# Hybrid encoder block on one core: row buffers, weight fetches and the first gated table of the head loop rearranged

## The chip, the cores and the metric

The kernel runs on one core of a Trainium2 chip. The metric is the device time of one execution in microseconds (us); lower is better. The core has a matrix engine (PE in the profile, with its weight loads shown apart as PEld), a vector engine (DVE), a scalar engine (ACT), a general engine (POOL) and a queue engine (SP) that issues most of the transfers. Each of them works through its own list of instructions strictly in order. An instruction that has to wait for another engine or a transfer holds up everything behind it on its own engine.

## The reference

The block prepends 16 learned tokens to a sequence of 1024 tokens of width 1024, applies two residual layers and a last normalization, and drops the learned tokens.

```
h = concat(meta, x)
h = h + token_mixer(rmsnorm(h))     # 4 gated (mLSTM) heads and 4 retention heads
h = h + channel_mixer(rmsnorm(h))   # silu(conv(u @ w_up)) * (u @ w_gate) @ w_down
out = rmsnorm(h)[:, 16:]
```

In the token mixer each of the eight heads has queries and keys of 128 columns, values of 256 columns and an output gate of 256 columns, all of them projections of the normalized input. A head's sequence is processed in chunks with a state carried from chunk to chunk. In a gated head the scores of a chunk are multiplied by a table of weights, exp(log gates), and q and k pass through a convolution over four tokens and a silu. In a retention head the table is a fixed decay, and q and k are rotated. Each head's result is normalized, multiplied by the gate, and all heads together are projected by w_out.

## The kernel before

Single-precision products are made of three reduced-precision ones: every operand is split into a rounded part (hi) and the remainder (lo), and PE computes hi*hi, hi*lo and lo*hi. So each weight block is fetched raw from memory, then **rounded**: ACT copies it to hi, and DVE subtracts to get lo (lines 151 and 152).

The heads run in the order 4, 0, 1, 2, 3, 5, 6, 7: first one retention head, then the four gated heads (0 to 3), then the other retention heads. For each head the program states three stages. In the **gate stage** (`o_group`) PE makes the output gate of the head in two blocks (o0, o1) of three token pieces each, and between these groups the head's scan over the first chunks is placed. In the **value stage** (`v_group`, nine chunks) PE makes the next head's values, and between them come the rest of the scan and `post_steps`: for each of three pieces a square root (line 891), the scaling of the rows (line 898), two transposes on PE (line 906) and the product with the gate. In the **query-key stage** (`qk_group`) PE makes the next head's queries and keys, three pieces each.

The scan step of a chunk (`scan_a`, `scan_b`) multiplies keys with queries on PE (line 796), transposes the keys (line 801), lets ACT scale and round the keys (`kwh`, line 809 in gated heads, 818 in retention heads) and DVE make the remainder (`kwl`), and multiplies both with the values on PE (lines 826 to 828), which gives the output of the chunk and the update of the state (`C`, line 868).

**Weights** come through one list of units, worked off in this order for each head: o0, o1, the rows of w_out for the last two tokens of the previous head (m0, m1), then v0, v1, q, k of the next head. `need(key, ahead)` makes sure that the unit `key` and the next `ahead` units of the list have been issued; to issue a weight unit means its fetch (line 148), and right behind it its rounding. Raw weights go to a ring of two buffers (pool `wraw`), rounded ones to a ring of three. The m units take a buffer of the same ring of two (line 177), are fetched by line 178 and used by DVE alone: each is multiplied into the accumulator `acc` of the last two tokens (lines 181 and 183). The value group of the first chunk (16 tokens) also reads the raw weights (line 367).

**Tables.** `tables(h)` fetches two tables: for a gated head A1 and A2 from a small matrix in memory, spread over all partitions (lines 531 and 532). For A1 POOL then adds the causal mask (lines 535 and 536), and ACT takes the exponential of nine chunks (line 539), the first of 16 columns and eight of 128. For the first gated head the call stands ahead of the head loop, and for the others behind the value stage of the head before.

**Order.** The program's text sets only a priority. A planner lays out each engine's list at build time: by its own estimates of durations it takes, for each engine, what would be ready, the earliest of the text first, subject to data, to buffers that come free, and to a few explicit rules, `after(x, y)`, which place x behind y on the same engine. There is such a rule for each square root of the heads before the last (behind the last gate's activation, line 431) and for the sigmoids of gated heads (behind the last silu).

Of the kernel before, what the change touches and what calls it, by code (L numbers as in the profile page):

```python
# [17 lines left out]
P = 128  # L18
# [6 lines left out]
H = 4  # L25
# [38 lines left out]
def body(ctx, tc, h_in, vecs, cst, mask_in, rot, w_v0, w_v, w_fm, w_out, w_up, w_gate, w_down, out):  # L64
# [56 lines left out]

    units = []
    ready = {}
    issued = [0]

    def unit(key, src, n):
        units.append((key, src, n))
# [4 lines left out]
    def split_tiles(nm):  # L132
        return [wsp.tile([P, UN], F32R, tag=t, name=f"{t}_{nm}") for t in ("hi", "lo")]

    def issue(upto):
        while issued[0] < min(upto, len(units)):
            u = units[issued[0]]
            issued[0] += 1
            if callable(u[1]):
                ready[u[0]] = u[1]()  # L140
                continue
            key, src, n = u
            nm = "_".join(str(k) for k in key)
            raw = raw_tile(nm)
            sub = 2 if key[:2] == ("v", HF) else 1
            cuts = [n * i // sub for i in range(sub + 1)]
            for c0, c1 in zip(cuts, cuts[1:]):
                last["raw"] = nc.sync.dma_start(raw[:, c0:c1], src[:, c0:c1])
            hi, lo = split_tiles(nm)
            for c0, c1 in zip(cuts, cuts[1:]):  # L150
                nc.scalar.copy(hi[:, c0:c1], raw[:, c0:c1])  # L151
                nc.vector.tensor_tensor(lo[:, c0:c1], raw[:, c0:c1], hi[:, c0:c1].bitcast(F32), ALU.subtract)  # L152
            ready[key] = (hi, lo, raw)

    order = {}

    def need(key, ahead):
        if not order:
            order.update({u[0]: i for i, u in enumerate(units)})
        issue(order[key] + 1 + ahead)  # L160
        return ready[key]


# [10 lines left out]
            unit((kind, h, b), w_fm[h, j + b], D)  # L174

    def last_two(k, raw=None):
        raw = raw_tile(f"m{k}") if raw is None else raw
        nc.sync.dma_start(raw[:, :D], w_out[k])
        for t in range(2):
            if k != 2 * HF:  # L180
                nc.vector.scalar_tensor_tensor(acc[:, t], raw[:, :D], mm[:, k, t:t + 1], acc[:, t], ALU.mult, ALU.add)
            else:
                nc.vector.tensor_scalar(acc[:, t], raw[:, :D], mm[:, k, t:t + 1], None, ALU.mult)
# [174 lines left out]
    def v_group(h, c, tag="pp"):  # L358
        t0, L = CH[c]
        nv = 264 if h == HF else 256  # L360
        U = [need(("v", h, i), 2 - i) for i in range(2)]
        pv = pp(f"pv{h}_{c}", tag)
        if c == 0:

            for i in range(2):
                for j in range(4):
                    nc.tensor.matmul(pv[32 * j:32 * j + 32, :nv], ug[:, 4 * i + j, :], U[i][2][:, j * nv:(j + 1) * nv],
                                     start=i == 0, stop=i == 1, tile_position=(0, 32 * j))
            t = wk.tile([P, WMAX], F32, tag="cv", name=f"v0_{h}", bufs=2)[:META]
            nc.scalar.copy(t[:, :nv], pv[:META, :nv])  # L370
            for j in range(1, 4):
                nc.vector.tensor_tensor(t[:, :nv], pv[32 * j:32 * j + META, :nv], t[:, :nv], ALU.add)
            return lambda: v_evac(h, 0, META, t)
        for kb in range(KB):
            hi, lo, _ = U[kb // 4]
            o = (kb % 4) * nv
            a, b = uh[kb][:, t0:t0 + L], ul[kb][:, t0:t0 + L]
            nc.tensor.matmul(pv[:L, :nv], a, hi[:, o:o + nv], start=kb == 0, stop=False)  # L378
            nc.tensor.matmul(pv[:L, :nv], a, lo[:, o:o + nv], start=False, stop=False)  # L379
            nc.tensor.matmul(pv[:L, :nv], b, hi[:, o:o + nv], start=False, stop=kb == KB - 1)  # L380
        return lambda: v_evac(h, c, L, pv)
# [40 lines left out]
    def o_group(h, b, p):  # L422
        t0, t1, _ = PIECES[p]
        t0 = max(t0, KEEP)
        n = t1 - t0
        U = need(("o", h, b), 2)
        pt = pp(f"po{h}_{b}_{p}")
        fm_mms(pt, U, t0, t1)
        s = sig(b, p)
        nc.vector.tensor_tensor(s, pt[:, :n], Rb[:, t0:t1], ALU.mult)  # L430
        x = nc.scalar.activation(s, s, AF.Sigmoid if h < H else AF.Silu)
        if h < H:
            after(x, last["silu"])
        last["gate"] = x
# [86 lines left out]
    def tables(h):  # L521
        if h > H + 1:
            return
        if h >= H:
            nc.sync.dma_start(A2, rot[:, 1])
            nc.sync.dma_start(A1, rot[:, 0])
            return
        src = scr.rearrange("x (c h) t -> x h c t", h=H)
        for x, a in ((0, A1), (1, A2)):
            if x == 0:  # L530
                nc.sync.dma_start(a[:, :META], src[x, h, 0, :META].partition_broadcast(P))
            nc.sync.dma_start(a[:, META:].rearrange("p (c t) -> p c t", t=P), src[x, h, 1:].partition_broadcast(P))
        m = mask
        a = A1[:, META:].rearrange("p (c t) -> p c t", t=P)
        nc.gpsimd.tensor_tensor(A1[:, :META], A1[:, :META], m[:, :META], ALU.add)
        nc.gpsimd.tensor_tensor(a, a, m.rearrange("p (o t) -> p o t", o=1).to_broadcast([P, NCH - 1, P]), ALU.add)
        for c in range(NCH):
            t0, L = CH[c]
            nc.scalar.activation(A1[:, t0:t0 + L], A1[:, t0:t0 + L], AF.Exp, bias=cols[:, 0, c * H + h:c * H + h + 1])

# [332 lines left out]
    def post_steps(h, p):  # L875
        t0, t1, chs = PIECES[p]
        n = len(chs)
        m = {}

        def stats():  # L880
            num, mv, base = outs.pop(p)
            z = mxp.tile([P, 4], F32, tag="z", name=f"z{h}_{p}", bufs=2)
            if h < H:
                den = base[:, 0:n, DV]
                e2 = cols[:, 2].rearrange("p (c h) -> p h c", h=H)[:, h, chs[0]:chs[0] + n]
                nc.vector.tensor_tensor(z[:, :n], den, den, ALU.mult)
                nc.vector.tensor_tensor(z[:, :n], z[:, :n], e2, ALU.max)
                nc.vector.scalar_tensor_tensor(z[:, :n], z[:, :n], EPS, mv[:, 0:n, 1], ALU.mult, ALU.add)
            else:
                nc.vector.tensor_tensor(z[:, :n], mv[:, 0:n, 1], Re[:, h - H, chs[0]:chs[0] + n], ALU.add)  # L890
            x = nc.scalar.activation(z[:, :n], z[:, :n], AF.Sqrt)
            if h < 7:
                after(x, last["gate"])
            nc.vector.reciprocal(z[:, :n], z[:, :n])
            nc.vector.scalar_tensor_tensor(mv[:, 0:n, 1], mv[:, 0:n, 0], -1.0, z[:, :n], ALU.mult, ALU.mult)
            for i, c in enumerate(chs):
                L = CH[c][1]
                nc.scalar.activation(num[i][:L, :DV], num[i][:L, :DV], AF.Identity, bias=mv[:L, i, 1:2], scale=z[:L, i:i + 1])
            m["num"] = num

        def half(b):
            num = m["num"]
            tr = ps.tile([P, 512], F32, tag="tr", name=f"tr{h}_{p}_{b}")
            for i, c in enumerate(chs):
                c0, L = CH[c]
                nc.tensor.transpose(tr[:, c0 - t0:c0 - t0 + L], num[i][:L, b * P:(b + 1) * P], ident[:L, :L])
            a0 = max(t0, KEEP)
            w = t1 - a0
            g = (V_MLG if h < H else V_RTG) + (h % H) * 2 + b
            i = 2 * h + b  # L910

            def mix_into(dst, x0, x1):
                nc.vector.scalar_tensor_tensor(dst, tr[:, x0 - t0:x1 - t0], vec[:, g:g + 1], sig(b, p)[:, x0 - a0:x1 - a0], ALU.mult, ALU.mult)
            if h == 7:
                for q, o in (("A2", MA), ("B2", MB)):
                    x0, x1 = max(a0, o), min(t1, o + HB)
                    if x0 < x1:
                        mix_into(wact(q, 6 + b)[:, x0 - o:x1 - o], x0, x1)
                if t1 > MB + HB:
                    mix_into(mm[:, i], MB + HB, t1)  # L920
                return
            mx = sig(b, p)
            mix_into(mx[:, :w], a0, t1)
            e = min(t1, MB + HB)
            nc.sync.dma_start(mxd[i][:, a0 - MA:e - MA], mx[:, :e - a0])
            if e < t1:
                nc.vector.tensor_copy(mm[:, i], mx[:, e - a0:w])
        return [stats, lambda: half(0), lambda: half(1)]
# [79 lines left out]
    for i, h in enumerate(ORDER):  # L1008
# [8 lines left out]
        merge([lambda c=c: (v_group(nxt, c)(), c == 4 and i == 4 and wsum_next()) for c in range(NCH)], side)  # L1017
        if i:
            tables(nxt)
        for kind in "qk":  # L1020
            for p in range(3):
                qk_group(nxt, kind, p)
# [585 lines left out]
```

## Time and profile before

| What | Value |
|---|---|
| median of three runs | 1547.7 us (1545.21, 1547.7, 1548.02) |
| the profiled execution, its own time | 1545.12 us |
| span of the profiled execution | 1543.3 us |
| PE busy | 1519.3 us (98%) |
| DVE busy / ACT busy | 1089.1 us (71%) / 732.0 us (47%) |
| mean granted clock of PE | 0.995 |

The span runs from the first to the last instruction of the execution; 1.8 us of its time lie around it. A list of waits names for each waiting instruction the engine, the program's name of what it writes and its line, then what released it; the numbers are the sum in us, how many times, and the longest. A timeline row has the start and the duration in us from the start of the span, then engine, line and operation, and in brackets the idle time of the engine just before it with what ended it. A row of windows has, for a stretch of time, its length, the busy time of each engine with the number of instructions, the granted clock of PE, the share of the transfer engines and GB/s.

### The profile page before, as it was taken

Reading aid. Unit: us, or ns where it says so; the run is one execution under the profiler, and the core shown is the slowest. Engines: PE = TensorE matmul, PEld = TensorE weight load, DVE = VectorE, ACT = ScalarE, POOL = GpSimd, SP = SyncE. Lnnn points to the kernel's source line nnn. Section 1 sums busy time; section 2 is a strip of 40 time slices with the busy share of each in tenths; the row PEclk is TensorE's granted clock in tenths of the full one; section 3 lists DMA queues with packets and bytes.
Section 4 is the critical chain, followed back from the end, with each engine's and each line's share of the span. In section 5 each row is a group of like instructions: output and inputs, shape, how many; then the busy total and the mean of one; then the engine's idle time right before and its main releaser. Section 6 shows DMA issues by size and latency. Waiting matters only on the chain.

```text
span 1543.3 us, 25397 instructions
## 1 busy us (share of the span) xinstructions
PE 1519.3 (98%) x9763; PEld 1397.2 (91%) x9763; DVE 1089.1 (71%) x2334; ACT 732.0 (47%) x1488; POOL 101.7 (7%) x117
## 2 busy tenths in 40 slices
PE   8999999999999999999999999999999999999997
PEld 8989999999999999997788998999999999888887
DVE  8757767676867566678867778776666666778657
ACT  7374554544543434436454465444444444434443
POOL 0001010010101000000000000211101110000000
PEclk9999999999999999999999999999999999999999
DMA  6125243452648143357543237889666667933313
GB/s 215 42 70 130 77 123 83 123 117 78 162 109 200 54 119 75 103 116 244 185 137 109 83 99 245 203 220 205 161 151 157 145 160 196 372 101 112 96 42 110
DMA packets 105192, 213.41 MB, mean 138 GB/s; under 512 B 9384, under 2 KB 31600, under 8 KB 105072
## 3 DMA queue, kind: packets, MB, share of 16 engines
q1 hardware_dynamic: 86384, 176.86, 33.8%
q0 software_dynamic: 18544, 34.87, 15.4%
q8 instruction: 76, 1.25, 0.3%
q14 instruction: 44, 0.36, 0.1%
q10 hardware_dynamic: 144, 0.07, 0.0%
HBM read 182.37 MB, written 84.19 MB: 173 GB/s over the span
## 4 chain that ended last, share of the span: by engine, by line
PE 94%; DVE 2%; DMA 2%; ACT 1%; issue 0%; POOL 0%; SPq 0%; DVEq 0%; ACTq 0%; POOLq 0%
PE pv L378 4%; PE pv L379 4%; PE pv L380 4%; PE po L388 4%; PE po L390 4%; PE po L389 4%; PE pdx L557 3%; PE pdx L559 3%; PE pdx L558 3%; PE pup_x L558 2%; PE pup_x L559 2%; PE pga_x L557 2%; PE pga_x L559 2%; PE pga_x L558 2%; PE pup_x L557 2%; PE pdy L557 2%
## 5 line engine op out<-in xcount | busy, mean ns | idle before, releaser
L378 PE MATMUL pv<-hi_v,uh 128*128 128x256 f32 (+1 forms) x512 | 147.5, 288 | 3.0 <-ACT hi_v L151 1.9
L379 PE MATMUL pv<-lo_v,uh 128*128 128x256 f32 (+1 forms) x512 | 146.4, 286 | 0.0
L380 PE MATMUL pv<-hi_v,ul 128*128 128x256 f32 (+1 forms) x512 | 145.3, 285 | 0.0
L388 PE MATMUL po<-uh,hi_o 128*128 128x386 f32 (+2 forms) x384 | 124.8, 325 | 0.0
L389 PE MATMUL po<-ul,hi_o 128*128 128x386 f32 (+2 forms) x384 | 123.4, 321 | 0.0
L390 PE MATMUL po<-uh,lo_o 128*128 128x386 f32 (+2 forms) x384 | 123.3, 321 | 0.0
L378 PEld LDWEIGHTS pv<-hi_v,uh 128*128 128x128 f32 x512 | 97.3, 190 | 6.6 <-issue 2.9
L379 PEld LDWEIGHTS pv<-lo_v,uh 128*128 128x128 f32 x512 | 97.1, 190 | 0.4 <-DVE lo_v L152 0.4
L380 PEld LDWEIGHTS pv<-hi_v,ul 128*128 128x128 f32 x512 | 97.0, 190 | 0.1
L196 POOL DMA_DIRECT2D wsd<-w_down_d x55 | 50.9, 1022 | 570.7 <-DMA wsd<-w_down_d 472.4
L245 ACT CAST hi_up<-raw_up 128x512 fp32r<-128x512 f32 (+1 forms) x52 | 36.5, 720 | 106.6 <-PE pga_z L558 61.2
L389 PEld LDWEIGHTS po<-ul,hi_o 128*128 128x128 f32 x384 | 73.0, 190 | 0.1
L388 PEld LDWEIGHTS po<-uh,hi_o 128*128 128x128 f32 x384 | 72.9, 190 | 0.1
L390 PEld LDWEIGHTS po<-uh,lo_o 128*128 128x128 f32 x384 | 72.8, 190 | 0.1
L246 DVE TENSOR_TENSOR lo_ga<-fraw_ga,hi_ga 128x512 fp32r<-128x512 f32 (+1 forms) x52 | 41.9, 809 | 37.9 <-ACT hi_ga L245 37.6
L557 PE MATMUL pup_x<-uh_g,hi_up 128*128 128x256 f32 (+1 forms) x240 | 67.2, 282 | 0.4 <-ACT uh_g L1039 0.4
L558 PE MATMUL pup_x<-ul_g,hi_up 128*128 128x256 f32 (+1 forms) x240 | 67.4, 283 | 0.1
L246 DVE TENSOR_TENSOR lo_up<-raw_up,hi_up 128x512 fp32r<-128x512 f32 (+1 forms) x52 | 41.4, 809 | 35.7 <-ACT hi_up L245 34.9
L559 PE MATMUL pup_x<-uh_g,lo_up 128*128 128x256 f32 (+1 forms) x240 | 66.3, 282 | 0.0
L388 PE MATMUL pq<-uh,hi_q 128*128 128x400 f32 (+2 forms) x192 | 62.4, 325 | 0.2 <-DVE rq L409 0.2
L388 PE MATMUL pk<-uh,hi_k 128*128 128x400 f32 (+2 forms) x192 | 62.4, 325 | 0.0
L389 PE MATMUL pk<-ul,hi_k 128*128 128x400 f32 (+2 forms) x192 | 62.2, 324 | 0.0
(751 smaller groups left out, 5027.3 us busy)
## 6 DMA issues: line engine op xcount, KB each, us to landing
raw_up<-w_up_d SPq DMA_DIRECT2D x22, 512.0 KB, 6.6
fraw_ga<-w_gate_d SPq DMA_DIRECT2D x22, 512.0 KB, 3.6
acts<-cv SPq DMA_DIRECT2D x44, 256.0 KB, 5.6
wsd<-w_down_d SPq DMA_DIRECT2D x22, 512.0 KB, 7.0
wsd<-w_down_d POOLq DMA_DIRECT2D x22, 512.0 KB, 6.6
rd<-wsd SPq DMA_DIRECT2D x22, 512.0 KB, 3.6
wsd<-w_down_d POOLq DMA_DIRECT2D x33, 256.0 KB, 7.2
raw_o<-w_fm_d SPq DMA_DIRECT2D x16, 512.0 KB, 3.6
```

What stands on the lines that cost most here:

```text
L196: nc.gpsimd.dma_start(x, v, accum_op=ALU.add)
L245: nc.scalar.copy(hi[:, o:o + n], x)
L246: nc.vector.tensor_tensor(lo[:, o:o + n], x, hi[:, o:o + n].bitcast(F32), ALU.subtract)
L378: nc.tensor.matmul(pv[:L, :nv], a, hi[:, o:o + nv], start=kb == 0, stop=False)
L379: nc.tensor.matmul(pv[:L, :nv], a, lo[:, o:o + nv], start=False, stop=False)
L380: nc.tensor.matmul(pv[:L, :nv], b, hi[:, o:o + nv], start=False, stop=kb == KB - 1)
L388: nc.tensor.matmul(pt[:, :n], a, uh[kb][:, t0:t1], start=kb == 0, stop=False)
L389: nc.tensor.matmul(pt[:, :n], a, ul[kb][:, t0:t1], start=False, stop=False)
L390: nc.tensor.matmul(pt[:, :n], b, uh[kb][:, t0:t1], start=False, stop=kb == KB - 1)
L557: m.append(nc.tensor.matmul(pt, ah, xh_, start=first and k == 0, stop=False, skip_group_check=True))
L558: nc.tensor.matmul(pt, ah, xl_, start=False, stop=False, skip_group_check=True)
L559: m.append(nc.tensor.matmul(pt, al, xh_, start=False, stop=last and k == n - 1, skip_group_check=True))
```

## The change

Three things are done.

1. **Row buffers.** The rows of w_out for the last two tokens (m units) no longer take a buffer of the ring of raw weights, but two of their own, one for even and one for odd rows. Those two buffers exist before too, for the sums of the first norm and for a ring of a later stage.
2. **Two points.** A new function `load(upto)` makes the fetches alone, and `issue` the rounding. `need` gets a third argument, the number of units ahead to be fetched. A value group asks for the fetch of three units past v0 and of two past v1 (so up to k), and for the rounding of one unit past v0 in the chunks 0 to 3, and of two (so q) from chunk 4 on; before it was two in each chunk. The groups of the second gate block ask from the second piece on for four units ahead, where they asked for two: m0, m1, v0 and v1.
3. **Exponentials.** The mask addition and the exponentials of a table are a function of their own, `exps(h)`. For the first gated head it is called behind the value stage of head 4, no longer ahead of the head loop; the fetch of the table stays where it was. For gated heads 1 to 3 it follows the fetch as before. And each exponential is bound by a rule behind the last square root that the text states ahead of it (`last["root"]`), in all four tables.

```
     issued, loaded, raws = [0], [0], {}
...
+    def load(upto):
+        while loaded[0] < min(upto, len(units)):
+            key, src = units[loaded[0]][:2]
+            loaded[0] += 1
+            if callable(src):
+                continue
+            n = units[loaded[0] - 1][2]
+            raws[key] = raw = raw_tile("_".join(str(k) for k in key))
+            sub = 2 if key[:2] == ("v", HF) else 1
+            cuts = [n * i // sub for i in range(sub + 1)]
+            for c0, c1 in zip(cuts, cuts[1:]):
+                last["raw"] = nc.sync.dma_start(raw[:, c0:c1], src[:, c0:c1])
...
+            load(issued[0])
...
-            raw = raw_tile(nm)
+            raw = raws.pop(key)
...
-            for c0, c1 in zip(cuts, cuts[1:]):
-                last["raw"] = nc.sync.dma_start(raw[:, c0:c1], src[:, c0:c1])
...
-    def need(key, ahead):
+    def need(key, ahead, loads=0):
...
         issue(order[key] + 1 + ahead)
+        if loads:
+            load(order[key] + 1 + loads)
...
     def last_two(k, raw=None):
-        raw = raw_tile(f"m{k}") if raw is None else raw
+        raw = accp.tile([P, 2 * HB], F32, tag=f"rr{k % 2}", name=f"raw_m{k}") if raw is None else raw
...
-        U = [need(("v", h, i), 2 - i) for i in range(2)]
+        U = [need(("v", h, i), (2 if c > 3 else 1) - i, 3 - i) for i in range(2)]
...
-        U = need(("o", h, b), 2)
+        U = need(("o", h, b), 4 if b and p else 2)
...
+        if h:
+            exps(h)
+
+    def exps(h):
         m = mask
...
-            nc.scalar.activation(A1[:, t0:t0 + L], A1[:, t0:t0 + L], AF.Exp, bias=cols[:, 0, c * H + h:c * H + h + 1])
+            after(nc.scalar.activation(A1[:, t0:t0 + L], A1[:, t0:t0 + L], AF.Exp, bias=cols[:, 0, c * H + h:c * H + h + 1]), last["root"])
...
-            x = nc.scalar.activation(z[:, :n], z[:, :n], AF.Sqrt)
+            x = last["root"] = nc.scalar.activation(z[:, :n], z[:, :n], AF.Sqrt)
...
         if i:
             tables(nxt)
+        else:
+            exps(nxt)
```

More of the change, by code (lines that the diff above doesn't have):

```diff
@@ L123, in body @@
     ready = {}
-    issued = [0]
+    issued, loaded, raws = [0], [0], {}
     def unit(key, src, n):
@@ L142, in issue @@
             key, src, n = u
-            nm = "_".join(str(k) for k in key)
-            raw = raw_tile(nm)
+            raw = raws.pop(key)
             sub = 2 if key[:2] == ("v", HF) else 1
             cuts = [n * i // sub for i in range(sub + 1)]
-            for c0, c1 in zip(cuts, cuts[1:]):
-                last["raw"] = nc.sync.dma_start(raw[:, c0:c1], src[:, c0:c1])
-            hi, lo = split_tiles(nm)
+            hi, lo = split_tiles("_".join(str(k) for k in key))
             for c0, c1 in zip(cuts, cuts[1:]):
```

## The prediction

> **What bounds the kernel now.** I read the page's busy table first, then the windows by stage, then PE's list of waits, and then the timelines around the two places that it names.
>
> ```profile
> span 1543.3 us, 25397 instructions
> PE 1519.3 (98%) x9763; PEld 1397.2 (91%) x9763; DVE 1089.1 (71%) x2334; ACT 732.0 (47%) x1488; POOL 101.7 (7%) x117
> ```
>
> PE is busy for 1519.3 of 1543.3 us. The change leaves every product in place, so it can only take from the 24.0 us in which PE is idle, or from time at a lower clock. The windows say where these lie: columns are the stretch, its length, then the busy time of PE, PEld, DVE, ACT and POOL, and the granted clock.
>
> ```profile
> 90.00:170.00 80.00, 76.70 (x562) 74.04 (x561) 56.63 (x153) 43.64 (x97) 7.92 (x7) 1.00 0.45 112
> 250.00:330.00 80.00, 80.00 (x588) 78.17 (x587) 54.95 (x154) 41.32 (x94) 6.44 (x6) 1.00 0.42 109
> 330.00:410.00 80.00, 77.16 (x557) 74.69 (x556) 53.22 (x152) 45.14 (x99) 6.92 (x7) 0.98 0.37 97
> 900.00:1543.00 643.00, 634.54 (x3746) 560.68 (x3744) 448.57 (x725) 290.03 (x523) 52.33 (x57) 1.00 0.60 166
> ```
>
> The change works in the head loop, some 64 to 740 us. There only two regions within its reach have holes: 3.3 us in 90 to 170 and 2.84 in 330 to 410 (with the clock at 0.98). The quiet stretch 250 to 330 shows that a whole head can pass without a hole. The 8.5 us behind 900 belong to other code. PE's waits name the holes:
>
> ```profile
> PE u L826 <- ACT kwh L809: 2.6, 1, 2.6
> PE u L826 <- DVE C L868: 1.3, 1, 1.3
> PE s L796 <- DVE kwl L819: 1.1, 1, 1.1
> PE pv L378 <- DVE gts L356: 1.0, 1, 1.0
> ```
>
> The first is in head 2's gate stage, the next two at the start of head 0's values, the fourth in the opening. The timeline of the second place:
>
> ```profile
> 97.04 2.38 POOL L536 TENSOR_TENSOR A<-A,mask 128x1024 f32<-128x1024 f32 x1 [9.49 <-DMA A<-scr]
> 98.22 1.05 ACT L151 CAST hi_q<-raw_q 128x1024 fp32r<-128x1024 f32 x1 [3.96 <-DMA raw_q<-w_fm_d]
> 99.28 1.28 ACT L539 ACT_TABLE_LOAD   x1
> 99.30 1.23 DVE L152 TENSOR_TENSOR lo_q<-raw_q,hi_q 128x1024 fp32r<-128x1024 f32 x1 [3.52 <-ACT hi_q L151]
> 100.58 2.45 ACT L539 ACTIVATE A<-A,cols 128x128 f32<-128x128 f32 x8
> 101.01 0.42 DVE L868 SCALAR_TENSOR_TENSOR C<-C,u 128x256 f32<-128x256 f32 x1
> 101.58 0.36 PE L826 MATMUL u<-vh,kwh 128*128 128x256 f32 x1 [1.27 <-DVE C L868]
> 102.93 0.35 ACT L818 ACTIVATE kwh<-s,Rc 128x128 fp32r<-128x128 f32 x1
> 103.72 0.49 PE L796 MATMUL s<-qT,kT 128*128 128x128 f32 x2 [1.07 <-DVE kwl L819]
> ```
>
> ACT stands 3.96 us before the rounding of q, whose raw weights are not there; DVE stands behind it at lo_q, with the state update C queued behind. PE runs dry for 1.27 us. Then ACT does a table load and eight exponentials (1.28 + 2.45 us), with the scan's kwh queued behind, and PE runs dry for another 1.07. The other place:
>
> ```profile
> 321.23 0.33 SPq L148 DMA_DIRECT2D raw_v<-w_v_d  x1
> 330.97 1.05 ACT L151 CAST hi_v<-raw_v 128x1024 fp32r<-128x1024 f32 x1 [13.44 <-DMA raw_v<-w_v_d]
> 331.93 0.53 ACT L415 ACTIVATE kT<-cvk 128x400 f32<-128x400 f32 x1
> 332.05 1.23 DVE L152 TENSOR_TENSOR lo_v<-raw_v,hi_v 128x1024 fp32r<-128x1024 f32 x1 [4.62 <-ACT hi_v L151]
> 336.96 1.28 ACT L431 ACT_TABLE_LOAD   x1
> 338.26 0.94 ACT L431 ACTIVATE sig<-sig 128x386 f32<-128x386 f32 x2
> 339.10 0.35 ACT L809 ACTIVATE kwh<-s,cols 128x128 fp32r<-128x128 f32 x1
> 339.50 0.39 PE L826 MATMUL u<-vh,kwh 128*128 128x258 f32 x1 [2.58 <-ACT kwh L809]
> 339.56 1.28 ACT L539 ACT_TABLE_LOAD   x1
> 340.85 0.31 ACT L539 ACTIVATE A<-A,cols 128x16 f32<-128x16 f32 x1
> 342.11 1.28 ACT L431 ACT_TABLE_LOAD   x1
> ```
>
> ACT waits 13.44 us for the raw values of the next head, DVE 4.62 us behind it; the silus of k, the gate's table load and kwh all come late, and PE waits 2.58 us. (The raw_v of the next head is fetched while the current head's keys are computed, long ahead of its place in the text: the planner runs ahead as far as buffers allow.)
>
> **The clock behind a hole.** Windows right after:
>
> ```profile
> 340.60:344.10 3.50, 3.50 (x13) 3.50 (x12) 1.56 (x2) 3.46 (x7) 0.00 (x0) 0.51 0.00 0
> 344.10:347.60 3.50, 3.50 (x26) 3.50 (x25) 2.97 (x11) 2.09 (x8) 0.00 (x0) 1.00 0.02 5
> ```
>
> For 3.5 us PE was granted 0.51 of its clock and started 13 products, where the next 3.5 us have 26. So the hole costs 3.5 x (1 - 0.51) = 1.7 us more. The Trainium skill (TensorE: Matmul & The Clock Gate, "Why this matters for your kernels") sets the limit at idle gaps of more than about 3 us; by it a hole of 2.58 us would cost only itself, and the sum below would be 1.7 less. The row shows the drop after the shorter hole, so I go by the row.
>
> **Part 1, row buffers.** Today m0 and m1 stand between o1 and v0 in the ring of two, so a value block can be fetched only when DVE has used up an m row; SP stands for that in its fetches (line 148) eleven times.
>
> ```profile
> SPq L148 <- DVE acc L181: 31.6, 11, 3.9
> 313.54 1.04 ACT L151 CAST hi_o<-raw_o 128x1024 fp32r<-128x1024 f32 x1
> 314.94 1.22 DVE L152 TENSOR_TENSOR lo_o<-raw_o,hi_o 128x1024 fp32r<-128x1024 f32 x1
> 323.66 0.34 PE L388 MATMUL po<-uh,hi_o 128*128 128x386 f32 x1
> ```
>
> With buffers of their own, v1 needs only o1's rounding, over at 314.94 + 1.22 = 316.2, and v0 that of o0, which is earlier still; today v0 goes out at 321.23. From issue to use it took 9.7 us today; even at that v0 would be there by about 326, at 316.2 issue, and it is likely earlier. Its rounded buffer is that of k, whose products run until the gate's begin at 323.66, so ACT's wait ends at some 324 to 326 in place of 331: 5 to 7 us earlier, and the chain silu, table load, kwh moves with it. That is more than the 2.58 us that PE waited. Removed: 2.58 and the 1.7 of clock. Lower end: nothing, if another fetch on SP's in-order queue takes the place. No bytes and no instructions are added, only other buffers. What is late next is the piece-by-piece arrival of k from DVE, which the quiet heads show to be covered.
>
> **Part 2, two points.** At 98 us q loses its early place in the text: its rounding is stated at chunk 4, while C of chunk 1 is stated ahead. The planner may still put hi_q into an ACT gap, but DVE should take C ahead of lo_q. I count the 1.27 us as removed; lower end 0 (hi_q and lo_q stay where they are), upper end 1.27. The move of v0 and v1 up into the gate groups raises the rank of two roundings a head (1.05 us ACT and 1.23 DVE each, rows above); they ran there or earlier anyway. Cost 0; the bad end is a rival below. The fetches of q and k still leave when the first chunk has read v's raw buffers, so SP, with the stores and table fetches queued behind, waits there as today: 0. In the opening q's rounding also comes later: it can give back the 1.0 us wait for gts, or cost up to its own 1.05 + 1.23 us if PE then waits for q; I take 0.
>
> **Part 3, exponentials.** The eight exponentials leave 99.28 to 103.03, and kwh need not wait for them: 1.07 us removed, the surest item. In the three other gated boundaries the 16-column exponential is today pulled into the gate stage (339.56 above) and costs ACT two table loads, 2 x 1.28; the rule puts it with the rest. PE does not wait for these two, so 0. What the rule adds is a block of 1.28 + 2.45 = 3.73 us behind the root:
>
> ```profile
> 311.46 0.20 ACT L891 ACTIVATE z<-z 128x2 f32<-128x2 f32 x1
> 312.54 1.10 ACT L898 ACTIVATE num<-num,mv,z 128x256 f32<-128x256 f32 x2 [0.69 <-DVE mv L895]
> 315.65 0.27 PE L906 MATMUL tr<-cs,num 128*128 128x128 f32 x1
> ```
>
> The cover is the 0.69 us gap and the 2.0 us between the end of L898 (313.64) and PE's transpose at 315.65. If all eight go ahead of L898, PE waits 3.73 - 0.69 - 2.0 = 1.0 us in a boundary; with four tables 4 us is the bad end, none the good one. L898 is stated ahead of the exponentials and is ready 0.9 us after the root, so I expect them mostly behind it, and allow 1.2 us for one boundary that is not. The Trainium skill (ScalarE: Activation LUTs, "What ACT_TABLE_LOAD costs") adds a drain of about 1.38 us to the load; by it the bad end would be 2.4 us a boundary. The rows have the exponential at 340.85 right behind a load of 1.28 begun at 339.56, so no drain is counted. POOL's mask addition can stay at 97 us, since nothing binds it to the root.
>
> **Sum.** 2.58 + 1.7 + 1.27 + 1.07 = 6.6 us gross, 1.2 back: 5.4 us. The profiled execution took 1545.12 us, so 1539.7. The runs' median is 2.6 us above the profiled time, two runs of three near 1548; I cannot see from one trace what the slower ones met, and carry half of it, 1.3: **1541.0 us**. A difference of 0.2% (3.1 us: below 1544.6 or above 1550.8) is about what a measurement tells from none.
>
> **Rivals.** *Only the first boundary gains*: raw_v stays late, since SP, in order, still waits for stores of finished heads ahead of it. For it: SP also waits long for things other than m; against it: v0's place in the ring is free 5 us earlier. 1545.1 - 2.3 + 1.3 = 1544.1.
>
> *Nothing moves*: the planner already runs ahead of the text by tens of us, so where the text states the rounding hardly matters, and holes of this size only wander. 1545.1 + 1.3 = 1546.4, up to the median.
>
> *The exponentials reach PE* in all four boundaries, each time 1.0 us, and each with the clock's 1.7: 10.8 us of cost against 6.6 gained, 1545.1 + 4.2 + 1.3 = 1550.6; without the clock 1543.8. Taken as 1547.
>
> *Slower: values rounded early block ACT.* Now of higher rank in the gate stage, v1's rounding needs the buffer that the gate products of o0 hold; placed too early, ACT stands there and the scan's kwh stands behind it, in seven heads.
>
> ```profile
> ACT hi_v L151 <- PE po L389: 5.8, 4, 2.3
> ```
>
> At the longest such wait, 2.3 us, passed on to PE in full: 7 x 2.3 = 16.1, and 1545.1 - 6.6 + 16.1 + 1.3 = 1555.9. It decides from 1.6 us a head (11 us). Against it: today these waits exist four times and PE's list has none from them.
>
> **Chances.** Forecast 0.45 (own range 1537 to 1544.6), only the first boundary 0.15, nothing 0.17, exponentials 0.08, slower 0.15. Faster by over 0.2%: nearly all of the first and two thirds of the second, 0.53; within: 0.27; slower: the last and scraps, 0.20. Low end 1537: all 6.6 and the 1.3 not carried, 1538.5, with 1.0 from the opening. High end 1550 takes in the next three cases; it leaves out the last.
>
> **What would show it.** No 13 us wait of ACT for raw_v; PE's waits without kwh L809 at head 2 and without C and kwl at 101 to 104; a granted clock of 1.00 in head 2; half the table loads of L539 (8 to 4). The prediction is wrong if new holes of over 1 us stand at the transposes L906 or at kwh in the gate stages, or if fetches of raw_v still leave after 320 us in head 2's place.

## The result, and the profile after

The changed kernel took 1553.93 us (median of five runs, 1551.61 to 1556.28), the kernel before beside it 1546.16 us (five runs, 1542.08 to 1548.02). The ratio on record is 1.0057, with a 95% interval of 1.0045 to 1.0068 (the two medians alone give 1.0050): slower, clear of noise, and above the range of 1537 to 1550. The profiled execution of the changed kernel has a span of 1550.2 us.

The head loop did what was forecast; the loss came behind it. Windows of the changed kernel (stretch, length, busy time of PE, PEld, DVE, ACT, POOL, granted clock):

```profile
90.00:170.00 80.00, 77.30 (x566) 74.45 (x566) 56.80 (x155) 42.01 (x97) 6.34 (x5) 1.00 0.40 110
330.00:410.00 80.00, 80.00 (x593) 78.14 (x592) 55.57 (x159) 41.36 (x96) 7.27 (x7) 1.00 0.41 105
650.00:740.00 90.00, 83.49 (x467) 73.66 (x466) 71.58 (x161) 40.06 (x84) 4.65 (x5) 0.98 0.59 178
740.00:850.00 110.00, 106.39 (x471) 84.87 (x470) 79.54 (x119) 51.83 (x87) 0.00 (x0) 1.00 0.37 128
```

The last two stretches in the kernel before:

```profile
650.00:740.00 90.00, 87.32 (x507) 78.67 (x506) 71.19 (x164) 40.72 (x85) 3.58 (x4) 0.98 0.56 165
740.00:850.00 110.00, 110.00 (x514) 90.49 (x512) 86.91 (x134) 55.73 (x97) 0.00 (x0) 1.00 0.44 149
```

The hole in head 2 (330 to 410) is gone, with its half clock. Between 650 and 850 us PE is idle for 6.51 + 3.61 = 10.1 us, where it was idle for 2.7. Most of that is the output projection (names with pw and w). The prediction named only two regions with holes up to 740 us; the first of these two rows, with 2.7 us idle and the clock at 0.98, is a third, and the loss falls right there. Two marks say how much it costs: the last gate products and the first products of the gated MLP, by their first and last starts in the listings of one line. Before:

```profile
L388 PE MATMUL po<-uh,hi_o x384: 275/337/527, 64.7 to 694.9; 128*128 128x386 f32 x64, 128*128 128x384 f32 x64, 128*128 128x256 f32 x64
L557 PE MATMUL pup<-xh,hi_up x48: 276/282/365, 858.6 to 915.2; 128*128 128x256 f32 x24, 128*128 128x258 f32 x24
```

and after:

```profile
L401 PE MATMUL po<-uh,hi_o x384: 276/336/426, 65.4 to 690.2; 128*128 128x386 f32 x64, 128*128 128x384 f32 x64, 128*128 128x256 f32 x64
L574 PE MATMUL pup<-xh,hi_up x48: 275/282/364, 864.7 to 921.6; 128*128 128x256 f32 x24, 128*128 128x258 f32 x24
```

The changed kernel is 694.9 - 690.2 = 4.7 us ahead at the end of the gates, and 864.7 - 858.6 = 6.1 us behind where the MLP begins: 10.8 us lost in between, 7.4 of them as added idle time of PE. In the 3.4 us that are left PE counts as busy, with 779 products between the marks before and after; the trace doesn't say why they took longer. What it waits for, from PE's list of waits after:

```profile
PE pwx L574 <- ACT hi_w L258: 4.5, 7, 0.9
PE tr L923 <- issue: 1.8, 1, 1.8
PE u L843 <- ACT vh L366: 1.7, 1, 1.7
PE pwx L576 <- DVE lo_w L259: 1.0, 1, 1.0
PE pwy L574 <- ACT hi_w L258: 0.7, 1, 0.7
```

Nine times PE waits for the rounding of an output weight: eight times for hi_w, once for lo_w, 6.2 us in all. The timeline of the changed kernel shows why that rounding is late:

```profile
638.52 0.33 SPq L247 DMA_DIRECT2D raw_up<-w_up_d  x1
651.46 0.42 SPq L247 DMA_DIRECT2D raw_up<-w_up_d  x1
660.36 1.05 ACT L258 CAST hi_up<-raw_up 128x1024 fp32r<-128x1024 f32 x1 [10.81 <-PE pk L402]
673.51 1.05 ACT L258 CAST hi_up<-raw_up 128x1024 fp32r<-128x1024 f32 x1 [1.75 <-PE po L402]
721.43 1.04 ACT L258 CAST hi_w<-raw_w 128x1024 fp32r<-128x1024 f32 x1 [1.86 <-PE pwx L575]
722.52 0.50 PE L574 MATMUL pwx<-rr,hi_w 128*128 128x512 f32 x1 [0.67 <-ACT hi_w L258]
728.16 1.04 ACT L258 CAST hi_w<-raw_w 128x1024 fp32r<-128x1024 f32 x1 [0.85 <-PE pwx L575]
729.26 0.50 PE L574 MATMUL pwx<-wtk,hi_w 128*128 128x512 f32 x1 [0.68 <-ACT hi_w L258]
```

The same fetch in the kernel before:

```profile
731.00 0.33 SPq L234 DMA_DIRECT2D raw_up<-w_up_d  x1
743.42 0.39 SPq L234 DMA_DIRECT2D raw_up<-w_up_d  x1
```

The first two weight blocks of the MLP (`up`, 0) are fetched 92 us earlier and rounded at 660 and 674 us, in the last head. Their first product comes at 864.7. Until then they hold two of the three rounded buffers. Each output weight then has the one buffer left: ACT waits for PE's last product with the old weight, rounds for 1.04 us, and PE waits for ACT. The last head's gate groups asked for them: behind o1 of the last head the list of units has m0 and m1, and then no v0 and v1 but the MLP's blocks, so "four ahead" reaches into them.

### The profile page after: what moved, and what is told of

Its sections match the earlier page's. It is cut to its first block, busy times and chain, and to the rows that moved or that the text cites. A ratio compares the mean times of both kernels' runs of the same rounds, so it can differ in the third digit from the quotient of the medians.

```text
span 1550.2 us, 25387 instructions
## 1 busy us (share of the span) xinstructions
PE 1521.0 (98%) x9763; PEld 1395.3 (90%) x9763; DVE 1091.5 (70%) x2334; ACT 722.3 (47%) x1480; POOL 101.1 (7%) x117
## 4 chain that ended last, share of the span: by engine, by line
PE 92%; DMA 3%; DVE 3%; ACT 1%; issue 1%; SPq 0%; DVEq 0%; ACTq 0%
PE po L401 4%; PE po L403 4%; PE po L402 4%; PE pv L391 4%; PE pv L392 3%; PE pv L393 3%; PE pdx L574 3%; PE pdx L576 3%; PE pdx L575 3%; PE pup_x L575 2%; PE pup_x L576 2%; PE pga_x L574 2%; PE pga_x L576 2%; PE pga_x L575 2%; PE pup_x L574 2%; PE pdy L574 2%
## 5 line engine op out<-in xcount | busy, mean ns | idle before, releaser
L209 POOL DMA_DIRECT2D wsw<-w_out_d x40 | 37.2, 1028 | 410.2 <-DMA wsw<-w_out_d 374.8
```

The costliest lines, as they stand in the source:

```text
L209: nc.gpsimd.dma_start(x, v, accum_op=ALU.add)
```

## The experiments

Every run was timed in five rounds beside the kernel before. Ratios are to the kernel before on the same chip, whose median was 1543.1 to 1545.8 us in these sets.

**1. The last head asks for two.**

```
-        U = need(("o", h, b), 4 if b and p else 2)
+        U = need(("o", h, b), 4 if b and p and h < 7 else 2)
```

> The changed kernel, but in the last head the second gate block asks for two units ahead as before; heads before it keep four. Theory R (ring): behind the last head's gate and row units the list of units goes on with the first two weight blocks of the gated MLP, so four ahead rounds these in the head loop, and they hold two of the three rounded buffers through the whole output projection, where PE then waits for hi_w. By R the loss is gone and the 4.7 us that the changed kernel was ahead at the end of the heads stay: 1541 to 1542 us beside 1546 of before, and no wait of PE for hi_w L258. Rival M (row buffers): the two buffers of the row units are those that the output projection later uses for its rounded activations, and the loss comes from them or from the moved exponentials: the time stays at 1552 to 1555.

Measured: 1541.23 us, ratio 0.9990 (0.9981 to 1.0000), where the change as a whole had 1.0057. No wait for hi_w is left in its list, and the window from 740 to 850 is full again:

```profile
740.00:850.00 110.00, 110.00 (x538) 91.48 (x537) 82.15 (x129) 53.07 (x95) 0.00 (x0) 1.00 0.40 133
```

**2. That alone, in the kernel before.**

```
-        U = need(("o", h, b), 2)
+        U = need(("o", h, b), 4 if b and p and h == 7 else 2)
```

> The kernel before, with one edit: in the last head alone the second gate block asks for four units ahead from its second piece on. Row buffers, fetches and exponentials are as before. R: the whole loss and none of the gain, 1546 + 11 = 1557 us (1553 to 1559), with PE waiting for hi_w some seven times. M: nothing, 1546.

Measured: 1558.19 us, ratio 1.0092 (1.0079 to 1.0105). The waits are those of the changed kernel:

```profile
PE pwx L557 <- ACT hi_w L245: 4.4, 6, 1.0
PE u L826 <- ACT kwh L809: 2.6, 1, 2.6
```

So the one number in the last head makes the loss, with no other part of the change present (head 2's old wait for kwh is still there). Rival M, row buffers or exponentials, falls with runs 1 and 2.

**3. One block instead of two.**

```
-        U = need(("o", h, b), 4 if b and p else 2)
+        U = need(("o", h, b), (4 if h < 7 else 3) if b and p else 2)
```

> The changed kernel, with three units ahead in the last head instead of four: only one of the two MLP blocks is rounded early and one of three rounded buffers is held. R: between the two, 1542 to 1549 us; with two buffers left for the projection's weights most waits for hi_w should go, so I expect nearer the low end, 1543 to 1545. M: 1552 to 1555 as in the changed kernel.

Measured: 1550.44 us, ratio 1.0050 (1.0035 to 1.0065). It lies between run 1 and the changed kernel, but above the range expected and near the high end, not the low one: one held buffer of three costs most of what two cost. Its waits are fewer and longer, and ACT now waits for fetches of raw output weights as well:

```profile
PE pwx L574 <- ACT hi_w L258: 3.6, 2, 3.0
732.70 1.05 ACT L258 CAST hi_w<-raw_w 128x1024 fp32r<-128x1024 f32 x1 [2.56 <-DMA raw_w<-wsw]
```

Part of the time is the clock: from 690 to 790 us the profiled execution of this run has three stretches of 3.4 us at half clock (694, 715 and 749 us), that of the changed kernel one (713 us). Why the fetches come late with one buffer held stays open, so this run alone doesn't show that a held buffer is all that it pays for.

**4. The buffers held, nothing fetched.** In the kernel of run 1:

```
+        if h == 7 and b and p == 1:
+            for j in range(2):
+                held.append(split_tiles(f"held{j}"))
+                for y in held[-1]:
+                    nc.vector.memset(y[:, :1].bitcast(F32), 0.0)
...
+    for j in range(2):
+        for i, y in enumerate(held[j]):
+            after(nc.vector.tensor_copy(scrap[:, 2 * j + i:2 * j + i + 1], y[:, :1].bitcast(F32)), last["rsplit"][1])
     for mb in (0, 1):
         need(("up", 0, mb), 0)
```

> The kernel of the first of these runs (two ahead in the last head), and in its last gate stage two pairs of the rounded ring are taken by tiles into which only one column of zeros is written, and which are read once behind the last roundings of the output projection. No MLP weight is fetched or rounded early: only the buffers are held. R, in the form that the rounded buffers are what matters: the loss is back, 1550 to 1555 us, with PE waiting for hi_w. Rival F (fetch): it was the early fetch, which takes raw buffers and a place in SP's order ahead of the projection's weights; then the time stays at that of the first run, 1541 to 1543.

Measured: 1556.49 us, ratio 1.0083 (1.0071 to 1.0096), somewhat above the range expected, with the waits for hi_w and lo_w back, and a new one for C:

```profile
PE pwx L582 <- ACT hi_w L258: 3.8, 5, 0.9
PE n L851 <- DVE C L893: 2.5, 1, 2.5
PE pwx L584 <- DVE lo_w L259: 1.4, 2, 1.0
```

Held buffers suffice: no early fetch and no early rounding of an MLP weight is needed for the loss. Rival F falls.

Runs 2 and 4 lose 14 to 15 us, the change itself some 10 (its ratio is 1.0057, that of run 1 is 0.9990). In the profiled executions two more stretches of 3.4 us at half clock go with this: between 690 and 850 us run 2 has three (two from 698 us on, one at 719) and run 4 three (two from 713 us on, one at 839), the changed kernel one (713 us). Run 4 also waits 2.5 us for C, which the changed kernel doesn't, so its loss is not of the held buffers' waits for hi_w and lo_w alone.

**5. to 8. What the parts of the repaired kernel do.** Run 5 is run 1 with the row units back in the ring:

```
-        raw = accp.tile([P, 2 * HB], F32, tag=f"rr{k % 2}", name=f"raw_m{k}") if raw is None else raw
+        raw = raw_tile(f"m{k}") if raw is None else raw
```

> The repaired kernel (two ahead in the last head), with the row units back in the ring of raw weights; two points and exponentials stay. Theory B (the row buffers removed head 2's hole): ACT's 13 us wait for raw_v and PE's wait for kwh in head 2 are back, 2.6 us and 1.7 of clock: 1543 to 1546 beside 1541.2. Rival T (the table loads that the moved exponentials took out of the gate stage removed it): no such wait, 1541.

Run 6 is run 1 with the exponentials as before:

```
-        if h:
+        if True:
             exps(h)
...
-            after(nc.scalar.activation(A1[:, t0:t0 + L], ...), last["root"])
+            nc.scalar.activation(A1[:, t0:t0 + L], ...)
...
-        else:
-            exps(nxt)
```

> The repaired kernel with the exponentials as before: the first gated head's ahead of the head loop, and no rule behind the root in any head. Eight table loads of L539's kind instead of four. Theory E (as predicted): the eight exponentials are back between the products at some 100 us and cost PE about 1.1 us there; nothing else: 1542 to 1543. By T above also head 2's hole is back: 1545.

Run 7 takes the fetch and rounding points of before (`2 - i` in the value groups, 2 in the gate groups), with row buffers and exponentials as changed:

```
-        U = [need(("v", h, i), (2 if c > 3 else 1) - i, 3 - i) for i in range(2)]
+        U = [need(("v", h, i), 2 - i) for i in range(2)]
...
-        U = need(("o", h, b), 4 if b and p else 2)
+        U = need(("o", h, b), 2)
```

> The kernel before with the row buffers and the moved exponentials alone: fetch and rounding at the points of before, two units ahead everywhere. As predicted, the second point frees C from behind the rounding of q at some 100 us, worth 1.3 us: so here PE's wait for C L868's kind is back, 1542.5. Rival S (the planner runs ahead of the text, so the points do nothing): 1541, and the rounding of q stands where it stands in the repaired kernel.

Run 8 is the changed kernel with only the second of these two edits.

> The changed kernel with the gate groups asking for two units ahead in every head; row buffers, exponentials and the value stage's two points stay. If the four ahead gain nothing in the heads where they were meant (v0 and v1 are rounded when a buffer comes free in any case): 1541, as the repaired kernel. If they do: 1543 or more.

Measured:

| Run | Median us | Ratio (95%) |
|---|---|---|
| 5 rows in the ring | 1543.0 | 0.9988 (0.9976 to 1.0000) |
| 6 exponentials as before | 1560.96 | 1.0105 (1.0087 to 1.0123) |
| 7 one point | 1541.32 | 0.9979 (0.9968 to 0.9991) |
| 8 two ahead everywhere | 1541.09 | 0.9979 (0.9967 to 0.9991) |

Run 5 has neither outcome that was expected. ACT's waits for raw_v are back, but short, and PE's wait for kwh in head 2 is not. Head 2 has another hole, 1.4 us at the transposes, behind nine exponentials that stand ahead of the scaling of the rows:

```profile
ACT hi_v L162 <- DMA raw_v<-w_v_d: 7.5, 5, 2.7
PE tr L923 <- ACT num L915: 2.0, 4, 1.4
397.84 2.65 ACT L556 ACTIVATE A<-A,cols 128x16 f32<-128x16 f32 x9
400.59 1.10 ACT L915 ACTIVATE num<-num,mv,z 128x256 f32<-128x256 f32 x2
```

Runs 7 and 8 agree: beside row buffers the second point of the value stage does nothing that shows, and rival S holds there. Run 8 is no slower than run 1, so the four ahead gain nothing in the other heads either. Runs 7 and 8 beat the kernel before by 0.2%, and the changed kernel by far.

Run 6 came out 16 to 19 us above what its two theories had. Its list of waits, and its timeline in the gate stage of head 1:

```profile
PE n L843 <- ACT num L877: 12.7, 4, 5.7
ACT A L556 <- POOL A L552: 16.5, 3, 7.0
237.06 1.22 SPq L207 DMA_DIRECT2D wsw<-w_out_d  x2
261.28 0.81 POOL L209 DMA_DIRECT2D wsw<-w_out_d  x1 [3.48 <-DMA wsw<-w_out_d]
261.82 0.52 POOL L552 TENSOR_TENSOR A<-A,mask 128x16 f32<-128x16 f32 x1
262.38 0.31 ACT L556 ACTIVATE A<-A,cols 128x16 f32<-128x16 f32 x1 [6.01 <-POOL A L552]
266.10 0.58 PE L843 MATMUL n<-vh,pt_1h 128*128 128x258 f32 x1 [5.18 <-ACT num L877]
```

The planner left the 16-column exponential in the gate stage, as before. But POOL was still summing blocks of w_out (`wsw`), ahead of the mask addition on its list; ACT stood 6.0 us for it, and PE 5.2 us for ACT.

**9. and 10. Rows alone, exponentials alone, in the kernel before.** Run 9 has this one edit:

```
-        raw = raw_tile(f"m{k}") if raw is None else raw
+        raw = accp.tile([P, 2 * HB], F32, tag=f"rr{k % 2}", name=f"raw_m{k}") if raw is None else raw
```

> The kernel before with the row buffers alone: one line. Theory G: with the values fetched earlier, the planner leaves the 16-column exponential of the next table in the gate stage, where its mask addition stands on POOL behind the sums of w_out; only the rule behind the root keeps it away. By G this kernel has the 5 us waits of PE for num that the kernel with the exponentials as before showed: 1556 to 1562. Rival P (the row buffers are the gain, the rest is neutral, and the slow result with the exponentials as before came from the two points): 1541.

Run 10 has the edits of `tables`, `exps` and the root, and nothing else.

> The kernel before with the exponentials alone, moved and bound behind the root; row units in the ring, one point. If they remove only their own hole at 103 us: 1 us off the kernel before. If they are also what freed head 2, as the run with the rows in the ring suggests (its head 2 has 1.4 us idle, the kernel before 2.8): 2 to 3 us off, and no half clock in head 2.

Measured: run 9 1542.89 us, ratio 0.9994 (0.9982 to 1.0006); run 10 1542.95 us, ratio 0.9987 (0.9975 to 0.9998). Theory G falls: the row buffers alone bring no wait for POOL. Rival P, 1541, isn't borne out either: the interval of run 9 includes no change at all. The row buffers alone close head 2's hole, and the exponentials alone do not. Head 2 in run 9, then in run 10:

```profile
330.00:410.00 80.00, 80.00 (x593) 78.17 (x592) 55.66 (x160) 44.47 (x98) 7.25 (x7) 1.00 0.41 107
```

```profile
330.00:410.00 80.00, 78.10 (x569) 75.91 (x568) 52.30 (x151) 42.07 (x96) 7.25 (x7) 0.98 0.41 102
ACT hi_v L162 <- DMA raw_v<-w_v_d: 41.9, 7, 14.5
```

The last row, of run 10, beside that of run 5 shows what the points do without row buffers. Run 5 has the exponentials and the ring of run 10, and also the two points and four units ahead in the heads before the last: there the longest wait for raw_v is 2.7 us, not 14.5, and PE's wait for kwh in head 2 is gone. So these earlier requests and the row buffers are two ways to the same end.

**11. Run 6 with two ahead.**

```
-        U = need(("o", h, b), 4 if b and p and h < 7 else 2)
+        U = need(("o", h, b), 2)
```

> The kernel with the exponentials as before, and the gate groups asking for two units ahead everywhere; row buffers and the value stage's two points stay. Theory W (the sums come late): with four ahead the text fetches v0 and v1 ahead of the sums of w_out, whose fetch is bound behind the last raw fetch stated; so the sums leave some 17 us later, POOL is busy with them when the 16-column mask addition of the next table is due, ACT waits for it in the gate stage and PE for ACT. With two ahead the sums leave early again: 1541.5 to 1544 us, no wait of ACT for POOL of over 1 us, and PE's holes at some 101 to 104 us as in the kernel before. Rival V (it is the value stage's two points): it stays at 1556 to 1563.

Measured: 1542.93 us, ratio 0.9987 (0.9975 to 0.9999). The sums of w_out leave early again, 18 us ahead of run 6, and the long wait for POOL is gone:

```profile
219.23 1.22 SPq L207 DMA_DIRECT2D wsw<-w_out_d  x2
ACT A L556 <- POOL A L553: 0.5, 1, 0.5
```

Theory W holds. The text binds the fetch of the sums behind the last raw fetch stated (`last["raw"]`). With four ahead that is v1's, which must wait for a buffer. The changed kernel has this delay too; it is harmless there only because the rule behind the root keeps the exponential out of the gate stage.

## Why the prediction was wrong

**The step that failed** is in part 2: "The move of v0 and v1 up into the gate groups raises the rank of two roundings a head ...; they ran there or earlier anyway. Cost 0". It put this term at nothing because it took the list of units as the same in every head. In the last head the units behind m0 and m1 are the MLP's first two blocks, which did not run there before: rounded 190 us ahead of use, they hold two of three buffers through the whole output projection. In place of 0 this costs some 10 us in the change itself (ratio 1.0057, against 0.9990 in run 1), and 14 to 15 us in runs 2 and 4 (1558.19 and 1556.49, against 1543.1 before and 1541.2 in run 1). The prediction stopped at 740 us because "the change works in the head loop"; the list of units runs on past it. One of its own signs of being wrong did show, a new hole of over 1 us at the transposes (tr L923, 1.8 us, at 711.8 us), but during the output projection; run 1 is without it.

**Slower, but not by the rival named.** The rival had values rounded early in seven heads, with ACT standing before a held buffer and kwh behind it. That wait hardly changed, 5.4 us in four waits against 5.8. Early rounding was the right kind of danger, in the wrong place: those who need the buffer later pay, not ACT in the gate stage. That the rival's 1555.9 lies near the measured 1553.93 is luck.

**Row buffers: right.** ACT's waits for raw_v are gone; it waits for PE's products with k instead, as worked out. v0's fetch leaves at 302.64 and v1's at 317.56 (forecast: v1 from 316.2; before: 321 and 327). After:

```profile
ACT hi_v L162 <- PE pk L402: 33.3, 4, 10.8
302.64 0.79 SPq L146 DMA_DIRECT2D raw_v<-w_v_d  x1
317.56 0.33 SPq L146 DMA_DIRECT2D raw_v<-w_v_d  x1
```

Head 2's 2.58 us and its half clock went, and run 9 shows that the row buffers alone do it; by run 5 the earlier requests can do it without them. The sums in medians are smaller than the 4.3 us priced from the trace: run 9 is 0.9 us below its before, an interval that reaches past none.

**Two points: wrong in effect.** The 1.27 us at 101 us were counted as removed because DVE would take C ahead of lo_q. It did not. After:

```profile
99.33 1.05 ACT L162 CAST hi_q<-raw_q 128x1024 fp32r<-128x1024 f32 x1 [4.37 <-DMA raw_q<-w_fm_d]
100.42 1.28 DVE L163 TENSOR_TENSOR lo_q<-raw_q,hi_q 128x1024 fp32r<-128x1024 f32 x1 [3.92 <-ACT hi_q L162]
102.19 0.42 DVE L885 SCALAR_TENSOR_TENSOR C<-C,u 128x256 f32<-128x256 f32 x1
102.19 0.51 ACT L366 ACTIVATE vh<-v,Rc 16x256 fp32r<-16x256 f32 x1 [0.51 <-DVE v L385]
102.75 0.35 PE L843 MATMUL u<-vh,kwh 128*128 128x256 f32 x1 [1.74 <-ACT vh L366]
```

C still stands behind lo_q, and so does DVE's v, for which ACT's vh and then PE wait. One hole of 1.74 us stands where two of 1.27 and 1.07 stood: 0.6 us gained in place of 2.34. The lower end of that term ("hi_q and lo_q stay where they are") was the true one. The 0.6 belongs to the exponentials: run 7, without the second point, has the same one hole (1.4 us), and so has run 10, with the exponentials alone (1.1 us), while run 11, with both points and the exponentials as before, has two (1.6 us for C, 1.0 for kwl).

**Exponentials: the hiding was right, the order not.** They were expected mostly behind L898 (now L915). All nine went ahead of it:

```profile
310.20 1.28 ACT L556 ACT_TABLE_LOAD   x1
311.50 2.65 ACT L556 ACTIVATE A<-A,cols 128x16 f32<-128x16 f32 x9
314.24 1.09 ACT L915 ACTIVATE num<-num,mv,z 128x256 f32<-128x256 f32 x2
```

PE has no hole in this head, so the bad end of 1.0 us a boundary did not come here: PE's first transpose stands at 316.14, 6.0 us behind the end of the root, where it was 4.0 before. That the planner moved it because it knew of the block is likely, but not shown. It isn't always enough: in run 5 the same order cost PE the 1.4 us shown above. The loads halved as said, from eight (L539) to four (L556).

**The base.** Half of the 2.6 us between the median and the profiled execution was carried. Further runs of the kernel before had medians of 1543.1 to 1545.8, so the profiled 1545.12 was not low, and nothing should have been carried. The repaired kernels come to 1541.1 to 1541.3, near the 1541.0 forecast, but as 0.1 to 0.2% below their before and not 0.4%: a hole in one profiled execution is not a gain of its size in the median.

## What to carry to other kernels

When work is asked for "n ahead" on a list, read what stands n ahead at the end of the loop too: the units behind the last turn belong to another stage. A rounded or prefetched tile costs its buffer from then until its last use, and with a ring of three, two tiles held by a later stage leave that ring without overlap. Where a rule binds something to "the last one stated", moving a fetch earlier in the text delays whatever is bound behind it.

## What the runs showed of the hardware

The spread between runs of the same kernel goes with PE's granted clock. In the twelve runs of run 1, the four at a mean of 0.993 took 1543.77 to 1544.4 us and the four at 0.997 or 0.998 took 1539.08 to 1540.01:

```
mean clock   time, us (run 1)
0.998        1539.75, 1540.01
0.997        1539.08, 1539.3
0.993        1543.77, 1543.8, 1543.88, 1544.4
```

That is 4.4 us, not far from the 5.4 us that were forecast as gain. One execution doesn't fit: in run 4 one at a mean of 0.941 took 1556.5 us, as one at 0.994 did (1556.49). A stretch of 3.4 us at half clock costs 1.7 us, 0.001 of the mean, so the step from 0.998 to 0.993 is worth four or five such stretches, an estimate from these numbers. The profiled execution of run 8 has no such stretch before its end, and the one of the changed kernel has two, one of them in the opening (34.0 to 37.4 us at 0.52) behind a wait of 1.8 us for gts. A hole isn't always needed: in run 7 PE is busy throughout from 820 to 832 us, and its granted clock is 0.60 from 823 to 827 us and 0.64 from 827 to 832, while products one column wide (pe, 32 of them from 821.5 to 826.3 us) run. What sets it off was not tested by itself.
